# Loading a norm's weight as one row and spreading it over the partitions with TensorE

## The chip, the cores and the metric

The kernel runs on one core of a Trainium2 chip. The time is the device time of one execution in microseconds (us). The core has five engines that run side by side and wait for one another through semaphores: TensorE (PE in the profile; PEld is its loading of weights), VectorE (DVE), ScalarE (ACT), GpSimd (POOL) and SyncE (SP). DMA transfers are issued from the queues of SP, ACT and POOL. A tensor in on-chip memory has 128 partitions; PE writes its results to eight banks of 128 x 512 F32 values, which ACT and DVE can read.

## The reference

One decoder layer for a prompt of 1024 tokens and eight single sample tokens that share weights, 1032 tokens in all, with a model width of 1024. The part that the change touches is the first norm and what uses it at once:

```python
def rmsnorm(x, g):
    xf = x.astype(jnp.float32)
    y = xf * lax.rsqrt(jnp.mean(xf * xf, axis=-1, keepdims=True) + EPS)
    return (y * g.astype(jnp.float32)).astype(x.dtype)

def decoder_layer(x, ...):
    h = rmsnorm(x, g_attn_norm)
    z = h @ w_in
    ...
```

`g_attn_norm` is one vector of 1024 values; every token's row is multiplied by it. `z` has 4360 columns, which are the queries, keys and values of a windowed attention and of a matrix-memory branch (mLSTM), its two gates, and the merge gates. After that come the two branches, their projections and merge, a residual add, a second norm, a gated feed-forward part (1024 to 2816 and back), another residual add and a final norm. The outputs are the normed tokens, the last keys and values, and the states of the matrix memory.

## The kernel before, in words

The 1032 tokens are cut into nine tiles of rows: eight of 128 tokens and one of 8. Tile t is loaded as `x{t}`, [128 tokens, 1024]. The norm of a tile is made in four steps, which are functions of their own:

- `norm_a`: ACT squares the tile and sums each row (`xq`, with the sum in `xss`). `rstd` then makes the mean plus epsilon on DVE (TENSOR_SCALAR) and raises it to the power -0.5 on POOL.
- `norm_b`: one DVE instruction multiplies the tile by its row's factor and by the norm's weight. For that the weight must stand in every partition: `gbc` is a tile [128, 1024] whose rows are all `g_attn`.
- `norm_t`: PE transposes the eight 128 x 128 blocks of the tile against the identity (`cst`, `ident`), four into each of two banks (`xT`).
- `norm_c`: each bank is split into a high and a low part, so that later products can be made in three passes of a shorter format: ACT writes the high part `hh` from the bank, DVE the rest `hl`.

Projections are computed with weights as the stationary operand and the transposed tokens as the moving one, in three chunks of 344 tokens, so that chunk 0 needs tiles 0, 1 and 2. The first product is that of the two mLSTM gates (`if`, the weights are split by ACT into `wl_if`, by DVE into the rest, and spread out by POOL into `wh_if`), the next are `mq` and `mk`.

`start` writes the beginning. SP's queue gets, in this order, tile 0, the weight `gbc`, tiles 1 to 3, and then slices of `w_in` alternating with the tiles 4 to 8. The load of `gbc` reads the one row of 4 KB from memory 128 times:

```python
        for t in range(4):
            x_load(t)
            if t == 0:
                sp.dma_start(gbc, g_attn[0].partition_broadcast(P))
```

Tiles 0, 1 and 2 are normed at once, and the tiles 3 to 8 are normed between the products of the first projections (`side`). While PE has nothing to do, `keep_warm(n)` gives it n products of a tile of zeros (`wz`, 128 x 512, BF16) whose result nobody reads; here they are called fillers. `WARM` holds their numbers: 22 before the first transposes, 3 behind tile 0's, 3 behind tile 1's, 4 behind tile 2's.

PE, SP and POOL take instructions in the order in which the program writes them. The order on ACT and DVE is set by a scheduler. The banks come from pools: `ps_g` (three, for projections and the fillers), `ps_a` (three) and `ps_t` (two).

Of the kernel before, what the change touches and what calls it, by code (L numbers as in the profile page):

```python
# [15 lines left out]
ALU = mybir.AluOpType  # L16
# [4 lines left out]
P = 128  # L21
D = 1024
# [19 lines left out]
PER_M = 4.85  # L42
Z_OFF = [0, 1, 2, 3, 2, 4, 0]
LAST = (4, 5)
WARM = (22, 3, 3, 4)
START = 4
PER_A = 2.95
AHEAD = 3
# [36 lines left out]
def decoder_step(ctx, tc, x_prompt, x_sample, cache_k, cache_v, st_c, st_n, st_m, rel_bias, w_in, b_if, sinks,  # L85
# [3 lines left out]
    pe, act, dve, pool, sp = nc.tensor, nc.scalar, nc.vector, nc.gpsimd, nc.sync  # L89
# [16 lines left out]
    def U(name, dt=F32, shape=None):  # L106
        return up.tile(shape or [P, NT], dt, tag="u", name=name)

    def T(name, shape, dt=F32):
        return tp.tile(shape, dt, tag="t", name=name)  # L110
# [4 lines left out]
    def ps_g(name):  # L115
        return pg.tile([P, 512], F32, tag="g", name=name)
# [17 lines left out]
    dve.memset(nhalf, -0.5)  # L134
    warm = kp.tile([P, 1], F32, name="warm")
    dve.memset(warm, 0.0)
    act.dma_start(cst[:, 0:P], c0[:, 0:P])
    act.activation(warm, warm, AF.Exp)
    gbc = U("gbc", shape=[P, D])
    wz = ep.tile([P, 512], BF16, name="wz")  # L140
    dve.memset(wz, 0.0)
    wps = ps_g("warm")
# [1 line left out]
    def keep_warm(n):  # L144
        for _ in range(n):
            pe.matmul(wps, wz[:, 0:P], wz, start=True, stop=True)

    keep_warm(WARM[0])

    def x_load(t):  # L150
        xt = U(f"x{t}", shape=[P, D])
        sp.dma_start(xt[0:rows[t], :], x_tok[t])
        xs.append(xt)
# [146 lines left out]
    def start(tiles):  # L300
        sl = [p[0] for t in tiles for p in t.prods]
        queue = [w for w in sl if not w.own]
        for t in range(4):
            x_load(t)
            if t == 0:
                sp.dma_start(gbc, g_attn[0].partition_broadcast(P))
        for i in range(FIRST):
            sl[i].load()
            x_load(4 + i)
        x_load(8)  # L310
        loads, splits = queue[2:], queue[2:]
        norm_a(0)
        norm_b(0)
        norm_a(1)
        v0 = norm_t(0)
        keep_warm(WARM[1])
        norm_b(1)
        v1 = norm_t(1)
        keep_warm(WARM[2])
        norm_a(2)  # L320
        norm_c(0, v0)
        norm_b(2)
        v2 = norm_t(2)
        keep_warm(WARM[3])
        norm_c(1, v1)
        sl[0].split()
        norm_c(2, v2)
        sl[1].split()
        loads.pop(0).load()
        loads.pop(0).load()  # L330
        side.add(skewed([(t,) for t in range(3, NB + 1)], [norm_a, norm_b, norm_t, norm_c], [0, 1, 2, 3]), small_loads())
        return sl, loads, splits
# [63 lines left out]
    def norm_a(t):  # L396
        n = rows[t]
        ss = S("xss", [P, 1], 4)
        jk = T(f"xq{t}", [P, D], BF16)
        act.activation(jk[0:n, :], xs[t][0:n, :], AF.Square, accum_out=ss[0:n, :])  # L400
        rstd(ss[0:n, :])
        xs[t] = (xs[t], ss)

    def norm_b(t, _=None):
        n = rows[t]
        xt, ss = xs[t]
        dve.scalar_tensor_tensor(out=xt[0:n, :], in0=xt[0:n, :], scalar=ss[0:n, 0:1], in1=gbc[0:n, :], op0=ALU.mult, op1=ALU.mult)

    def norm_t(t, _=None):
        n = rows[t]  # L410
        xt = xs[t][0]
        vs = []
        for g in range(2):
            tps = (ps_t if t % 2 else ps_a)(f"xT{t}_{g}")
            v = tps.rearrange("p (k t) -> p k t", k=4)[:, :, 0:n]
            for j in range(4):
                pe.transpose(v[:, j], xt[0:n, (4 * g + j) * P:(4 * g + j + 1) * P], ident[0:n, 0:n])
            vs.append(v)
        return vs

    def norm_c(t, vs):
        ts_ = slice(t * P, t * P + rows[t])
        for g in range(2):
            split(hhw[g][:, :, ts_], hlw[g][:, :, ts_], vs[g])
# [330 lines left out]
    def small_loads():  # L755
        pool.dma_start(cst[:, P:], c0[:, P:])
        pool.dma_start(graw[0:8, :], g_ffn.rearrange("o (k p) -> (o k) p", p=P))
        pool.dma_start(graw[8:12, :], g_head.rearrange("o (k p) -> (o k) p", p=P))
        oh = T("oh", [33, 512])
        pool.dma_start(oh, c1)  # L760
        rows_in.append(oh)
        pool.memset(rb[32:33, :], 1.0)
        pool.dma_start(rb[0:32, :], rel_bias)
        pool.dma_start(sink, sinks[0].partition_broadcast(P))
        pool.memset(rst[0:4, :], 1.0)
        pool.memset(rst[0:4, 0:NP].rearrange("p (c t) -> p c t", t=P)[:, :, 0:1], 0.0)
        pool.memset(rw, 0.0)
        pool.dma_start(samp[0], rep(st_n[0].rearrange("b h d -> (b h) d"), 64))
        pool.dma_start(samp[1][:, 2:3], rep(st_m[0].rearrange("b (h o) -> (b h) o", o=1), 1))
        pool.dma_start(sinks_s, sinks[0].rearrange("(h o) -> h o", o=1).unsqueeze(0).to_broadcast([NS, 8, 1]))  # L770
        yield
# [137 lines left out]
    def skewed(units, stages, offs):  # L909
        st = {}  # L910
        for t in range(len(units) + max(offs)):
            for o, f in zip(offs, stages):
                if 0 <= t - o < len(units):
                    u = units[t - o]
                    st[u] = f(*u, st[u]) if u in st else f(*u)
                    yield
# [993 lines left out]
    def hooks_of(i, preps=True):  # L1910
# [12 lines left out]
        if i < NM - 2 and i % 2 == 0 and i >= 2 or i == NM - 1:  # L1923
            def start(i=i):
                p = (KeptPair if i == NM - 1 else Pair)((i - 2) // 2, VL[(i - 2) // 2 * 2], VL[(i - 2) // 2 * 2 + 1])
                main_line(p.s0)
                for j, s in zip(range(2, 7), (p.s1, p.s2, p.s3, p.s4, p.s5)):
                    hk[j].append(ml(s))
            hk[1].append(start)
        if i in (NM, NM + 1):  # L1930
            def start(i=i):
                a, b = u_split(VL[i - 2])
                hk[2].append(ml(a))
                hk[3].append(ml(b))
            hk[1].append(start)
# [176 lines left out]
    for t in tiles[2:FIRST]:  # L2112
        t.prods[0][0].own = True
    run(tiles[:ngate], jobs, *start(tiles[:ngate]))
    gates()
    queue = [w for w in branch if not w.own][2:]
# [151 lines left out]
```

## Time and profile before

| what | before |
|---|---|
| median of 3 runs | 1391.66 us (1391.24 to 1391.66) |
| the profiled execution | 1391.65 us |
| its span | 1389.9 us |
| what lies around the span | 1.75 us |
| PE busy | 1369.4 us, 99% of the span |
| DVE busy | 975.4 us, 70% |
| ACT busy | 617.0 us, 44% |
| POOL busy | 242.0 us, 17% |
| first filler on PE starts | 1.25 us |
| first transposes start | 8.22 us |
| first gate products start | 15.51 us |
| load of `gbc`: issued, to landing | 1.18 us, 5.3 us |

The span is the time from the first to the last recorded instruction; the profiled execution's own time is a little longer. In a view in order of time each row has its start and length in us, the engine, the line of the kernel, the operation, the tile written and the tiles read (buffer numbers left out), their sizes, how many instructions are merged in the row, and in brackets how long the engine had been idle before it and what ended that idle time. The chain of waits follows the work that ended last back to its start. A row of a DMA queue gives packets, MB moved and the share of the 16 DMA engines. The engines PE and PEld are pipelined, so that ends of PE's rows are modelled.

### The profile page before, as it was taken

Reading aid. Unit: us, or ns where it says so; the run is one execution under the profiler, and the core shown is the slowest. Engines: PE = TensorE matmul, PEld = TensorE weight load, DVE = VectorE, ACT = ScalarE, POOL = GpSimd, SP = SyncE. Lnnn points to the kernel's source line nnn. Section 1 sums busy time; section 2 is a strip of 40 time slices with the busy share of each in tenths; the row PEclk is TensorE's granted clock in tenths of the full one; section 3 lists DMA queues with packets and bytes.
Section 4 is the critical chain, followed back from the end, with each engine's and each line's share of the span. In section 5 each row is a group of like instructions: output and inputs, shape, how many; then the busy total and the mean of one; then the engine's idle time right before and its main releaser. Section 6 shows DMA issues by size and latency. Waiting matters only on the chain.

```text
span 1389.9 us, 26966 instructions
## 1 busy us (share of the span) xinstructions
PE 1369.4 (99%) x10723; PEld 1337.9 (96%) x10724; DVE 975.4 (70%) x1853; ACT 617.0 (44%) x1407; POOL 242.0 (17%) x303
## 2 busy tenths in 40 slices
PE   9999999999999999999999999999999999999996
PEld 7999889999999999999999999999999999999996
DVE  7252758886944444755587888898888878888875
ACT  6243567654443331374454343444433343333325
POOL 4012111001111100001132232333333220000003
PEclk9999999999999999999999999999999999999998
DMA  7144224114233274788423344544434468677633
GB/s 224 32 117 113 62 63 100 31 62 149 81 107 100 84 283 137 221 281 283 166 77 120 110 153 153 168 168 139 131 114 144 146 214 304 220 239 237 221 123 122
DMA packets 179173, 208.42 MB, mean 150 GB/s; under 512 B 20638, under 2 KB 137634, under 8 KB 179032
## 3 DMA queue, kind: packets, MB, share of 16 engines
q1 hardware_dynamic: 161928, 151.72, 35.1%
q0 software_dynamic: 16688, 54.40, 10.7%
q8 instruction: 84, 1.38, 0.4%
q10 hardware_dynamic: 432, 0.59, 0.1%
q14 instruction: 41, 0.34, 0.1%
HBM read 140.31 MB, written 68.96 MB: 151 GB/s over the span
## 4 chain that ended last, share of the span: by engine, by line
PE 90%; DVE 3%; ACT 2%; DMA 2%; issue 1%; POOL 0%; SPq 0%; ACTq 0%; POOLq 0%; DVEq 0%
PE af L1589 18%; PE df L1589 9%; PE ad L1589 7%; PE wo L1261 6%; PE bf L1589 5%; PE ag L1589 4%; PE dd L1589 4%; PE o L226 3%; PE mv L226 3%; PE wm L1385 3%; PE wa L1385 3%; PE q L226 3%; PE dg L1589 2%; PE bd L1589 2%; PE mk L226 2%; PE gm L226 2%
## 5 line engine op out<-in xcount | busy, mean ns | idle before, releaser
L125 POOL TENSOR_TENSOR s1f<-s1f,R 128x516 f32<-128x516 f32 x42 | 68.8, 1637 | 87.2 <-DVE s1f L125 71.5
L1589 PE MATMUL df<-Th,op6f 128*128 128x258 f32 x352 | 67.3, 283 | 1.3 <-DVE uu L125 1.3
L1589 PE MATMUL af<-Th,op0f 128*128 128x258 f32 x352 | 67.4, 284 | 0.0
L1589 PE MATMUL bf<-Th,op2f 128*128 128x258 f32 x352 | 67.3, 283 | 0.0
L1589 PE MATMUL df<-Th,op4f 128*128 128x258 f32 x352 | 67.3, 284 | 0.0
L1589 PE MATMUL af<-Th,op1f 128*128 128x258 f32 x352 | 67.1, 283 | 0.0
L1589 PE MATMUL af<-Th,op3f 128*128 128x258 f32 x352 | 66.9, 283 | 0.0
L1589 PE MATMUL af<-Th,op5f 128*128 128x258 f32 x336 | 64.1, 283 | 0.0
L1625 ACT ACTIVATE s1f<-s1f 128x516 f32<-128x516 f32 (+1 forms) x23 | 14.2, 618 | 103.5 <-POOL s1f L125 103.5
L1589 PEld LDWEIGHTS df<-Th,op6f 128*128 128x128 f32 x352 | 55.9, 189 | 1.5 <-DVE uu L125 1.5
L1589 PEld LDWEIGHTS af<-Th,op1f 128*128 128x128 f32 x352 | 56.0, 189 | 0.0
L1589 PEld LDWEIGHTS af<-Th,op0f 128*128 128x128 f32 x352 | 56.0, 189 | 0.0
L1589 PEld LDWEIGHTS bf<-Th,op2f 128*128 128x128 f32 x352 | 56.0, 189 | 0.0
L1589 PEld LDWEIGHTS df<-Th,op4f 128*128 128x128 f32 x352 | 55.8, 189 | 0.0
L1589 PEld LDWEIGHTS af<-Th,op3f 128*128 128x128 f32 x352 | 55.6, 189 | 0.0
L1589 PEld LDWEIGHTS af<-Th,op5f 128*128 128x128 f32 x336 | 53.4, 190 | 0.0
L125 POOL TENSOR_TENSOR s2f<-s2f,R 128x516 f32<-128x516 f32 x21 | 27.4, 1307 | 135.5 <-ACT s2f L1625 135.4
L1589 PE MATMUL bf<-Tl,op2f 128*128 128x258 f32 x176 | 49.8, 283 | 0.0
L1589 PE MATMUL df<-Tl,op6f 128*128 128x258 f32 x176 | 49.7, 282 | 0.0
L1589 PE MATMUL af<-Tl,op1f 128*128 128x258 f32 x176 | 49.7, 282 | 0.0
L1589 PE MATMUL af<-Tl,op0f 128*128 128x258 f32 x176 | 49.7, 282 | 0.0
L1589 PE MATMUL df<-Tl,op4f 128*128 128x258 f32 x176 | 49.7, 282 | 0.0
(690 smaller groups left out, 4935.9 us busy)
## 6 DMA issues: line engine op xcount, KB each, us to landing
ta<-d_t SPq DMA_DIRECT2D x63, 516.0 KB, 6.6
Yd<-in_w_down_dram SPq DMA_DIRECT2D x40, 256.0 KB, 3.5
d_t<-h POOLq DMA_DIRECT2D x18, 516.0 KB, 5.2
d_t<-t POOLq DMA_DIRECT2D x18, 516.0 KB, 4.6
Xf<-in_w_gate_dram SPq DMA_DIRECT2D x22, 256.0 KB, 4.1
Xf<-in_w_up_dram SPq DMA_DIRECT2D x22, 256.0 KB, 6.9
Yf<-in_w_gate_dram SPq DMA_DIRECT2D x22, 256.0 KB, 3.0
Yf<-in_w_up_dram SPq DMA_DIRECT2D x22, 256.0 KB
```

The costliest lines, as they stand in the source:

```text
L125: return eng.tensor_tensor(out=out, in0=a, in1=b, op=op)
L226: pe.matmul(o, a[:, k, :], b[:, cs], start=(k == 0 and i == 0), stop=(k == n - 1 and i == len(passes) - 1))
L1261: pe.matmul(ps[:, th, 0:HB], a[:, k, :], b, start=(k == 0 and i == 0), stop=(k == KD - 1 and i == 2))
L1385: pe.matmul(ps[:, c, 0:CW], a[:, k, :], b[:, cs], start=(k == 0 and q == 0), stop=(k == 3 and q == 2))
L1589: pe.matmul(ps[:, s if ps.shape[1] > 1 else 0, 0:HB], a, b, start=(first and k == 0 and i == 0), stop=(k == self.nk - 1 and i == 2), skip_ ...
L1625: act.activation(s, s, AF.Silu)
```

## The change

The weight is no longer loaded into all partitions. ACT's queue loads it as one row into partition 0 of `gbc` (4 KB), ahead of the identity, and the load in SP's queue between the tiles 0 and 1 is left out. `one` is a row of 128 ones. Two F32 products of TensorE with `one` as the stationary operand and half of the row as the moving one give the weight in every partition, in two banks of `ps_g` (`gain0`, `gain1`). The 22 fillers before the first transposes become 4 ahead of these products and 9 behind them. `norm_b` of the tiles 0, 1 and 2 is made in two halves of 512 columns which read the banks; two ACT copies write the banks to `gbc`, which the tiles 3 to 8 read as before.

```diff
@@ -42,7 +42,7 @@
-WARM = (22, 3, 3, 4)
+WARM = (4, 9, 3, 3, 4)
@@ -134,9 +134,12 @@
     dve.memset(nhalf, -0.5)
     warm = kp.tile([P, 1], F32, name="warm")
     dve.memset(warm, 0.0)
+    gbc = U("gbc", shape=[P, D])
+    act.dma_start(gbc[0:1, :], g_attn)
+    one = T("one", [1, P])
+    dve.memset(one, 1.0)
     act.dma_start(cst[:, 0:P], c0[:, 0:P])
     act.activation(warm, warm, AF.Exp)
-    gbc = U("gbc", shape=[P, D])
     wz = ep.tile([P, 512], BF16, name="wz")
     dve.memset(wz, 0.0)
     wps = ps_g("warm")
@@ -146,6 +149,10 @@
     keep_warm(WARM[0])
+    gps = [ps_g(f"gain{i}") for i in range(2)]
+    for i in range(2):
+        pe.matmul(gps[i], one, gbc[0:1, i * 512:(i + 1) * 512], start=True, stop=True)
+    keep_warm(WARM[1])
@@ -302,8 +309,6 @@
         for t in range(4):
             x_load(t)
-            if t == 0:
-                sp.dma_start(gbc, g_attn[0].partition_broadcast(P))
@@ -313,15 +318,17 @@
         norm_b(0)
         norm_a(1)
         v0 = norm_t(0)
-        keep_warm(WARM[1])
+        keep_warm(WARM[2])
         norm_b(1)
         v1 = norm_t(1)
-        keep_warm(WARM[2])
+        keep_warm(WARM[3])
         norm_a(2)
         norm_c(0, v0)
         norm_b(2)
+        for i in range(2):
+            act.copy(gbc[:, i * 512:(i + 1) * 512], gps[i])
         v2 = norm_t(2)
-        keep_warm(WARM[3])
+        keep_warm(WARM[4])
@@ -404,6 +411,11 @@
     def norm_b(t, _=None):
         n = rows[t]
         xt, ss = xs[t]
+        if t < 3:
+            for i in range(2):
+                cs = slice(i * 512, (i + 1) * 512)
+                dve.scalar_tensor_tensor(out=xt[0:n, cs], in0=xt[0:n, cs], scalar=ss[0:n, 0:1], in1=gps[i], op0=ALU.mult, op1=ALU.mult)
+            return
         dve.scalar_tensor_tensor(out=xt[0:n, :], in0=xt[0:n, :], scalar=ss[0:n, 0:1], in1=gbc[0:n, :], op0=ALU.mult, op1=ALU.mult)
```

What the change does to the order of instructions stands here for the two places at which one engine waits for another. The numbers behind a name tell buffers apart and differ between the two programs. First DVE, from tile 0's norm to tile 1's split (`x_214`, `x_217`, `x_219` are tiles 0 to 2 before, `x_212`, `x_214`, `x_216` in the changed kernel). Before:

```order
L386 TENSOR_SCALAR xss<-xss 128x1
L407 SCALAR_TENSOR_TENSOR x_214<-x_214,xss,gbc 128x1024
L386 TENSOR_SCALAR xss<-xss 128x1
L407 SCALAR_TENSOR_TENSOR x_217<-x_217,xss,gbc 128x1024
L386 TENSOR_SCALAR xss<-xss 128x1
L125 TENSOR_TENSOR hl_126<-xT_0_252,hh_124 128x4x128
L125 TENSOR_TENSOR hl_127<-xT_1_257,hh_125 128x4x128
L407 SCALAR_TENSOR_TENSOR x_219<-x_219,xss,gbc 128x1024
```

In the changed kernel:

```order
L393 TENSOR_SCALAR xss<-xss 128x1
L417 SCALAR_TENSOR_TENSOR x_212<-x_212,xss,gain_109 128x512
L417 SCALAR_TENSOR_TENSOR x_212<-x_212,xss,gain_110 128x512
L393 TENSOR_SCALAR xss<-xss 128x1
L417 SCALAR_TENSOR_TENSOR x_214<-x_214,xss,gain_109 128x512
L417 SCALAR_TENSOR_TENSOR x_214<-x_214,xss,gain_110 128x512
L393 TENSOR_SCALAR xss<-xss 128x1
L125 TENSOR_TENSOR hl_124<-xT_0_250,hh_122 128x4x128
L125 TENSOR_TENSOR hl_125<-xT_1_255,hh_123 128x4x128
L417 SCALAR_TENSOR_TENSOR x_216<-x_216,xss,gain_109 128x512
L417 SCALAR_TENSOR_TENSOR x_216<-x_216,xss,gain_110 128x512
```

Each norm product of the three tiles is now two instructions of 512 columns that read a bank written by PE; the order is otherwise the same, here and in the rest of the program.

Then ACT, from tile 2's squares (`xq`) to tile 1's high parts (`hh`) and the gate weights. Before:

```order
L400 ACTIVATE xq_280,xss<-x_219 128x1024
L231 ACTIVATE hh_124<-xT_0_252 128x4x128
L231 ACTIVATE hh_125<-xT_1_257 128x4x128
L231 ACTIVATE hh_124<-xT_0_266 128x4x128
L231 ACTIVATE hh_125<-xT_1_271 128x4x128
L231 ACTIVATE wl_if<-ws_if 128x64
```

In the changed kernel:

```order
L407 ACTIVATE xq_279,xss<-x_216 128x1024
L238 ACTIVATE hh_122<-xT_0_250 128x4x128
L238 ACTIVATE hh_123<-xT_1_255 128x4x128
L329 COPY gbc<-gain_109 128x512
L329 COPY gbc<-gain_110 128x512
L238 ACTIVATE hh_122<-xT_0_265 128x4x128
L238 ACTIVATE hh_123<-xT_1_270 128x4x128
L238 ACTIVATE wl_if<-ws_if 128x64
```

The two copies from the banks to `gbc` stand between tile 0's and tile 1's high parts; at the beginning of ACT's order the load of `gbc` stands ahead of the load of the identity. On PE the two products (L154) stand behind the fourth filler, and nine fillers stand between them and tile 0's transposes. On every engine all that follows is the same row by row.

## The prediction

> **What bounds the kernel now.** I read the page's totals first, then the chain of waits over the first 60 us, then each engine in order of time up to 20 us.
>
> ```profile
> span 1389.9 us, 26966 instructions
> PE 1369.4 (99%) x10723; PEld 1337.9 (96%) x10724; DVE 975.4 (70%) x1853; ACT 617.0 (44%) x1407; POOL 242.0 (17%) x303
> ```
>
> PE is the bound nearly everywhere, so a change ahead of the first real product is worth what it moves the start of the unbroken PE stream. Where that stream starts, and what leads to it, stands in the chain (start, length, what):
>
> ```profile
> 1.18 0.42 SPq L306
> ...
> 1.65 6.28 DMA x<-in_x_prompt_dram
> ...
> 7.96 1.16 ACT xq L400 x2
> ...
> 9.96 1.28 DVE x L407
> ...
> 12.51 1.20 DVE x L407
> 13.71 0.04 issue
> 13.76 1.09 PE xT L417 x8
> 14.85 0.05 issue
> 14.90 0.81 PE warm L146 x3
> 15.71 2.60 PE if L218 x16
> ```
>
> The chain passes the issue of the gain load on SP's queue, waits for token tile 1, then goes through the norm of tiles 1 and 2 on DVE to the gate products at 15.71. From there PE is in the chain almost without a break. So the change has to be priced on the 15.7 us before that. DVE in order of time:
>
> ```profile
> 6.88 1.28 DVE L407 SCALAR_TENSOR_TENSOR x<-x,xss,gbc 128x1024 f32<-128x1024 f32 x1 [0.68 <-POOL xss L125]
> 9.14 0.15 DVE L386 TENSOR_SCALAR xss<-xss 128x1 f32<-128x1 f32 x1 [0.97 <-ACT xq L400]
> 9.96 1.28 DVE L407 SCALAR_TENSOR_TENSOR x<-x,xss,gbc 128x1024 f32<-128x1024 f32 x1 [0.67 <-POOL xss L125]
> ...
> 11.23 1.28 DVE L125 TENSOR_TENSOR hl<-xT,hh 128x512 fp32r<-128x512 f32 x2
> 12.43 1.27 DVE L407 SCALAR_TENSOR_TENSOR x<-x,xss,gbc 128x1024 f32<-128x1024 f32 x1
> 13.62 1.28 DVE L125 TENSOR_TENSOR hl<-xT,hh 128x512 fp32r<-128x512 f32 x2
> 14.82 0.22 DVE L125 TENSOR_TENSOR wl_if<-ws_if,wl_if 128x64 fp32r<-128x64 f32 x1
> ...
> 18.76 1.28 DVE L407 SCALAR_TENSOR_TENSOR x<-x,xss,gbc 128x1024 f32<-128x1024 f32 x1
> ```
>
> Two things: DVE idles 0.97 us before 9.14 because tile 1 came late; from 9.96 on it is busy without a gap, through the product of tile 2 and the split of the gate weights (wl_if). ACT and POOL in order of time:
>
> ```profile
> 4.87 1.06 ACT L400 ACTIVATE xq<-x 128x1024 bf16<-128x1024 f32 x1 [2.19 <-DMA x<-in_x_prompt_dram]
> ...
> 7.96 1.06 ACT L400 ACTIVATE xq<-x 128x1024 bf16<-128x1024 f32 x1 [1.94 <-DMA x<-in_x_prompt_dram]
> ...
> 9.23 1.06 ACT L400 ACTIVATE xq<-x 128x1024 bf16<-128x1024 f32 x1
> ...
> 10.29 1.06 ACT L231 ACTIVATE hh<-xT 128x512 fp32r<-128x512 f32 x2
> 12.00 1.08 ACT L231 ACTIVATE hh<-xT 128x512 fp32r<-128x512 f32 x2 [0.65 <-PE xT L417]
> ```
>
> ```profile
> 9.37 0.56 POOL L125 TENSOR_TENSOR xss<-xss,nhalf 128x1 f32<-128x1 f32 x1 [2.52 <-DVE xss L386]
> ...
> 15.10 0.36 POOL L255 CAST wh_if<-wl_if 128x32 fp32r<-128x32 f32 x2 [1.18 <-DVE wl_if L125]
> ```
>
> ACT waits for tile 0 until 4.87 and for tile 1 until 7.96. POOL's cast of the gate weights ends at 15.46, with the last filler of PE; both release the gate products.
>
> **Removed: 512 KB ahead of tile 1.** The gain load stands in SP's queue between tiles 0 and 1. What that queue (q1) had moved by 4.87 us (tile 0 landed), 6.5 (gain: issued at 1.18, 5.3 us to landing) and 7.93 (tile 1), as packets, MB, share, one row for each window from 0:
>
> ```profile
> q1 hardware_dynamic: 205, 0.77, 51.5%
> ```
>
> ```profile
> q1 hardware_dynamic: 336, 1.25, 58.2%
> ```
>
> ```profile
> q1 hardware_dynamic: 498, 1.84, 66.2%
> ```
>
> A 512 KB load is 0.524 MB. Tile 0 lands with 0.77 MB moved, the gain with 1.25 (1.05 needed), tile 1 with 1.84 (1.57 needed): each lands when the queue is 0.20 to 0.27 MB past it. Without the gain load tile 1 needs 1.25 to 1.3 MB and lands near 6.5 us instead of 7.93, tile 2 near 7.9. SP's issue of 0.42 us goes too. All later loads move up by the same 1.4 us; none of them bounds the stretch that follows.
>
> **Added on PE.** Before: 22 fillers. Now 4, two F32 products of one row of ones with the gain row, 9 fillers. The products wait for the row, and behind them in PE's order stand the fillers and tile 0's transposes; ACT and DVE wait for those. The fillers now, their pace (weight loads, start and length) and the first transposes:
>
> ```profile
> 1.25 7.10 PE L146 MATMUL warm<-wz 128*128 128x512 bf16 x22 [1.25 <-DVE wz L141]
> ...
> 5.49 0.15 PEld L146 LDWEIGHTS <-wz 128*128 128x128 bf16 x1 [0.28 <-issue]
> 5.81 2.04 PEld L146 LDWEIGHTS <-wz 128*128 128x128 bf16 x10 [0.17 <-issue]
> 8.22 0.86 PEld L417 LDWEIGHTS xT<-cst,x 128*128 128x128 f32 x8 [0.37 <-DVE x L407]
> ```
>
> A filler takes 0.43 us before 5.8 us (the 11 that start from 1.25), and 0.21 after it: the array runs at half pace at first. The granted clock in the windows reads 1.00 throughout and does not show this.
>
> The nearest F32 product in the trace is the bias table's, 384 columns as two rows at full pace:
>
> ```profile
> L779 PE MATMUL bt<-oh,rb x2: 483/484/486, 68.1 to 68.4; 33*8 33x384 f32 x2
> ```
>
> The two rows start 0.3 us apart and cover 0.8 us in all, about 0.65 of streaming and a tail of 0.16. For 512 columns that is 0.87 us of streaming at full pace, 1.74 at half.
>
> When does the row land? The load is issued first on ACT's queue, near 0.74 us. Bounds: two small gain loads on POOL's queue at 31.6 us took 2.0 to 2.3 us, hence 2.8 to 3.0; the two tiny bias loads on POOL's queue, issued in the same crowded start, took 5.4 to 6.0, hence 6.1 to 6.7. The rows of both, and of what ACT's queue (q10, the identity in 144 packets) had moved by 2.75 and by 4.87 us:
>
> ```profile
> DMA to landing us min/median/max: 2.0/2.1/2.3
> ```
>
> ```profile
> DMA to landing us min/median/max: 5.4/5.7/6.0
> ```
>
> ```profile
> q10 hardware_dynamic: 4, 0.00, 0.2%
> ```
>
> ```profile
> q10 hardware_dynamic: 144, 0.07, 4.6%
> ```
>
> The same queue's first packets passed just before 2.75 us, and the row now goes ahead of them: I take 3.2 us. Then the first product is done near 3.2+1.74+0.16 = 5.1, the second near 6.8 at half pace, 6.3 if the pace rises at 5.8 as now. DVE needs the first at 6.88 and the second at 7.5, so they cost nothing; the cover is 0.7 us. The 9 fillers (9x0.21 = 1.9 us) end between 8.2 and 8.7, where the 22 end now (8.2). ACT takes the transposes only when tile 2's squares are done, near 9.1, so up to 0.5 us of lateness is hidden.
>
> **Added on DVE and ACT.** The norm product of tiles 0 to 2 becomes two halves of 512 that read a bank. The nearest row with a bank as source is hl<-xT: 1.28 us for two of 512, the same as one of 1024 from memory. I price the split at 0. A gain: transposes 0 to 3 of a tile can start 0.64 us earlier. The copy of both banks to memory is two ACT copies of 512, about 1.06 us as hh<-xT for the same shape; they stand after tile 0's hh and before tile 1's hh, where ACT idles 0.65 us now. The matrix of the gain is needed in memory by tile 3 only (18.76 now, the copies end near 11.2). The memset of the ones (0.06 us on DVE) is before any work. ACT issues the identity's load and its table load one DMA issue (0.4 us) later; ACT waits 2.19 us for tile 0, and the identity, complete by 4.87 now, is needed at 8.2, so nothing.
>
> **Sum, in the order of time.** Tile 0's norm product starts at 6.88 as now and ends at 8.16. Tile 1's squares are done near 7.7, no longer late: DVE's next step starts at 8.16 instead of 9.14. It is now DVE that sets it, so of the 1.4 us won on the load 1.0 is left. POOL's power 8.35 to 8.9, tile 1's product 8.95 to 10.2 (9.96 now, -1.0). ACT: tile 2's squares 7.95 to 9.1, tile 0's hh 9.1 to 10.15. DVE: tile 0's hl 10.3 to 11.5, tile 2's product 11.5 to 12.75 (12.43 now, -0.95), tile 1's hl from 12.7; its hh is ready at 12.3 (transposes at 11.2, copies until 11.2, then 1.08), 0.4 us of cover for the copies. wl_if at 13.9 (14.82 now), POOL's cast done at 14.5, gate products at 14.55 instead of 15.51. PE is free by then: tile 2's transposes end near 13.3, the four fillers at 14.1. From 14.5 on the order of PE, DVE and ACT is the same row by row, so the 0.95 us stay.
>
> The profiled run took 1391.65 us, beside a median of 1391.66: one and the same. 1391.65 - 0.95 = 1390.7 us. Without the other terms the case runs from -0.3 (row at 4.5) to -1.5 (the load's whole gain).
>
> **Rivals.**
>
> 1. *PE reaches tile 0's transposes late* (slower). The place is the start of those transposes. Break-even: ACT's hh starts at 10.29 now, which half the transposes precede by 0.5 us, so from 9.7 on the gain is gone. Price by the late bound: row at 6.4, PE idle since 3.0 and so at half pace, products until 10.0, 9 fillers at first at half pace until 12.1, transposes until 12.9; hh starts near 12.6, tile 2's product near 14.6 instead of 12.43: about +2.1, 1393.7 us. With a row at 3.2 but half pace until 10, fillers end at 10.4 and the sum is about +0.3. For it: no product on PE waits for a load at this place now, and the half pace lasts until 5.8 as it is. Against: ACT's queue moves packets by 2.75.
> The Trainium skill ("TensorE: Matmul & The Clock Gate", Part 1: The HAM clock gate) says the pace doubles after a free-running window of about 3.4 us of sustained activity, and that idling loses it. By that rule a gap at 3.0 could push the rise to a later window, which is this rival's mild end (0.08 of its chance); the trace's rise at 5.81, 4.56 us after the first filler, fits it.
>
> 2. *The start moves and the end doesn't*: a wait later in the program that doesn't hang on the start takes the time back. The chain does hold long DMA waits:
>
> ```profile
> 147.64 6.83 DMA kq<-d_int
> ```
>
> But that one reads rows written by the kernel itself behind PE's products, so it moves along. Time: 1391.6.
>
> 3. *More than forecast*: if banks are read faster than memory and the earlier half transposes shift tile 0's and 2's splits too, the start moves by the queue's full 1.4 us and up to 0.6 for the halves: -2.0, 1389.6 us. Against: DVE's string of products doesn't shrink by any row here.
>
> **How the numbers follow.** Forecast 0.58, rival 1 0.2, rival 2 0.1, rival 3 0.12. The likeliest gives 1390.7, by itself 1390.1 to 1391.4. Taking in rival 2, rival 3 down to its middle and the mild half of rival 1: 1389.8 to 1392.6. A measurement of this kernel tells about 0.2%, 2.8 us, from no change. Every case priced above lies within that; beyond it are only a rival 1 worse than its late bound (0.04) and an effect that I don't see on the faster side (0.03). So faster 0.03, same 0.93, slower 0.04.
>
> **What would show it.** Right: tile 1's squares start near 6.5 and tile 1's product near 8.95, the gain products end before 7.5, transposes of tile 0 start before 9, gate products near 14.55, and one constant shift afterwards. Wrong: DVE waiting for PE (gain) before tile 0's product, fillers at 0.43 us behind the products, ACT's first hh after 10.3, or a shift that is not the same at 75 us and at the end.

## Result and the profile after

The changed kernel takes 1396.96 us (median of 6 runs, 1394.78 to 1398.54) beside 1391.66 us before (1390.88 to 1392.07 in the same comparison): a ratio of 1.0037, 95% interval 1.0024 to 1.0050. It is 5.3 us slower, where 1390.7 had been forecast and 1392.6 was the range's upper end. A second set of 6 runs of the same kernel gave 1395.40 beside 1392.01, 1.0030 (1.0018 to 1.0042): 3.4 us slower. The profiled execution of the changed kernel took 1395.29 us.

The page's totals after:

```profile
span 1393.1 us, 26972 instructions
PE 1372.9 (99%) x10718; PEld 1339.5 (96%) x10719; DVE 975.5 (70%) x1857; ACT 618.3 (44%) x1409; POOL 242.6 (17%) x303
```

PE has 3.5 us more busy time with 5 matmuls and 5 weight loads fewer, so some of its work went slower. Where is told by the chain of waits of the first 21 us (start, length, what):

```profile
1.38 1.89 PE warm L149 x4
3.27 3.71 PE gain L154 x4
6.97 3.95 PE warm L149 x9
10.93 1.72 PE xT L429 x8
...
12.67 0.61 ACT hh L238
...
13.91 1.41 DVE x L417 x2
...
15.34 0.58 ACT gbc L329
...
16.31 0.61 ACT hh L238
...
17.06 0.68 DVE hl L125
...
18.36 2.80 PE if L225 x16
```

The load of token tile 1, which led this chain before, is gone from it. PE leads it from the first filler to tile 0's transposes, then tile 2's norm product on DVE, then the copies of the gain on ACT. The same stretch by engine in order of time, PE and then DVE and ACT:

```profile
3.19 0.50 PEld L154 LDWEIGHTS gain<-gbc,one 1*128 1x128 f32 x2 [0.84 <-DMA gbc<-in_g_attn_norm_dram]
3.20 3.78 PE L154 MATMUL gain<-gbc,one 1*128 1x512 f32 x4
6.91 4.02 PE L149 MATMUL warm<-wz 128*128 128x512 bf16 x9
10.72 1.92 PE L429 MATMUL xT<-cst,x 128*128 128x128 f32 x8
...
18.36 1.53 PE L225 MATMUL if<-hh,wh_if 128*128 128x344 f32 x8 [1.41 <-POOL wh_if L262]
```

```profile
8.82 1.41 DVE L417 SCALAR_TENSOR_TENSOR x<-x,xss,gain 128x512 f32<-128x512 f32 x2 [0.67 <-POOL xss L125]
11.82 0.60 ACT L238 ACTIVATE hh<-xT 128x512 fp32r<-128x512 f32 x1 [2.79 <-PE xT L429]
13.91 1.40 DVE L417 SCALAR_TENSOR_TENSOR x<-x,xss,gain 128x512 f32<-128x512 f32 x2
14.68 1.24 ACT L329 COPY gbc<-gain 128x512 f32<-128x512 f32 x2 [1.41 <-DVE x L417]
16.45 1.29 DVE L125 TENSOR_TENSOR hl<-xT,hh 128x512 fp32r<-128x512 f32 x2 [1.15 <-ACT hh L238]
```

Three things are to be seen. The row of the gain lands at 3.19 and both products are done at 6.98. The nine fillers behind them take 4.02 us, 0.43 each, half pace, and tile 0's eight transposes are as slow (1.92 us instead of 1.09 at full pace); ACT waits 2.79 us for them and starts its first split at 11.82, 1.53 us later than before (10.29). Then ACT's copies stand at 14.68: they wait 1.41 us for DVE's norm product of tile 2, which reads the same banks, and tile 1's split stands behind them; DVE idles 1.15 us. The gate products start at 18.36 instead of 15.51.

So the start is 2.85 us late. Against the profile before, the same rows of PE (beginning of `gps`, 65.4 us before, and so on) are 2.8 us late at 65 us, 2.9 at 197, 3.2 from 497 us to the end; outside the span lie 2.2 us instead of 1.75. That is 3.6 us for this execution. The first set's median, 5.3 us, says that other executions lose more. The profiled execution of the second set (1398.51 us) shows where: 1.9 us late at 65, 3.5 at 197, 6.4 from 696 us on. The change also brought losses that come and go, hundreds of microseconds behind its place.

### The profile page after: what moved, and what is told of

Read it like the earlier page. It is cut to its first block, busy times and chain, and to the rows that moved or that the text cites. A ratio compares the mean times of both kernels' runs of the same rounds, so it can differ in the third digit from the quotient of the medians.

```text
span 1393.1 us, 26972 instructions
## 1 busy us (share of the span) xinstructions
PE 1372.9 (99%) x10718; PEld 1339.5 (96%) x10719; DVE 975.5 (70%) x1857; ACT 618.3 (44%) x1409; POOL 242.6 (17%) x303
## 4 chain that ended last, share of the span: by engine, by line
PE 91%; DVE 3%; ACT 2%; DMA 1%; issue 1%; POOL 0%; SPq 0%; ACTq 0%; POOLq 0%; DVEq 0%
PE af L1601 18%; PE df L1601 9%; PE ad L1601 7%; PE wo L1273 6%; PE bf L1601 5%; PE ag L1601 4%; PE dd L1601 4%; PE o L233 3%; PE mv L233 3%; PE wm L1397 3%; PE wa L1397 3%; PE q L233 3%; PE dg L1601 2%; PE bd L1601 2%; PE mk L233 2%; PE gm L233 2%
```

## Experiments

There were two theories at the outset. A: products of one row do not raise PE's pace, whatever their type; the half pace then lasts through fillers and transposes. B: F32 products (or the wait for their row) are what holds the pace, or the pace costs nothing and the copies are the loss. In the table, "gate" is the start of the gate products in the profiled execution (15.51 before), "at 65" how much later than before the row of `gps` starts there, "time" the median less that of the kernel before, run beside it. There is one profile for each row, so single places can differ from execution to execution, as the first two rows show.

| kernel | gate, us | at 65, us | time, us | ratio (95%) |
|---|---|---|---|---|
| the change | 18.36 | +2.8 | +5.3 | 1.0037 (1.0024 to 1.0050) |
| the change again | 17.43 | +1.9 | +3.4 | 1.0030 (1.0018 to 1.0042) |
| p1 one-row F32 stand-ins | 16.77 | +1.3 | +4.0 | 1.0026 (1.0017 to 1.0036) |
| p2 128-row F32 stand-ins | 15.43 | -0.1 | +3.9 | 1.0023 (1.0015 to 1.0032) |
| p3 one-row BF16 stand-ins | 15.61 | +0.1 | +0.5 | 1.0003 (0.9994 to 1.0011) |
| p4 64-row BF16 stand-ins | 16.24 | +0.7 | +0.3 | 1.0002 (0.9993 to 1.0011) |
| c1 copies late | 16.74 | +1.8 | +4.9 | 1.0033 (1.0020 to 1.0045) |
| c2 fillers first | 17.49 | +1.9 | +3.3 | 1.0025 (1.0015 to 1.0035) |
| c3 both | 15.33 | +0.4 | +4.4 | 1.0032 (1.0020 to 1.0043) |
| q1 before, 17 fillers | 15.52 | 0.0 | +1.9 | 1.0012 (1.0004 to 1.0021) |
| q2 p2, count restored | 15.50 | 0.0 | +0.3 | 1.0002 (0.9993 to 1.0011) |
| q3 change, count restored | 18.23 | +2.7 | +3.4 | 1.0023 (1.0014 to 1.0032) |
| q4 c3, count restored | 16.25 | +1.3 | +1.7 | 1.0013 (1.0004 to 1.0021) |
| r1 q3 with copies late | 16.61 | +1.6 | +2.7 | 1.0020 (1.0011 to 1.0030) |
| r2 r1, gain over 128 rows | 17.25 | +2.3 | +4.4 | 1.0030 (1.0020 to 1.0040) |
| r3 r2, row earlier | 15.28 | +0.3 | +1.7 | 1.0013 (1.0004 to 1.0022) |
| r4 before, 5 products more | 15.48 | 0.0 | -0.2 | 1.0000 (0.9991 to 1.0009) |

### The pace, with stand-ins in the kernel before

Four kernels are the kernel before with 4 fillers, then products of zeros where the gain products would stand, then 9 fillers. p1 and p2 also clear a tile of F32 zeros on DVE; nothing else differs.

p1, and p2 with `zf[:, 0:P], zf` in place of the one row:

```diff
-    keep_warm(WARM[0])
+    zf = ep.tile([P, 512], F32, name="zf")
+    dve.memset(zf, 0.0)
+    keep_warm(4)
+    for _ in range(2):
+        pe.matmul(wps, zf[0:1, 0:P], zf[0:1, :], start=True, stop=True)
+    keep_warm(9)
```

p3, and p4 with 64 rows:

```diff
-    keep_warm(WARM[0])
+    keep_warm(4)
+    for _ in range(8):
+        pe.matmul(wps, wz[0:1, 0:P], wz[0:1, :], start=True, stop=True)
+    keep_warm(9)
```

> The kernel before, with its 22 fillers replaced by 4 fillers, two F32 products of ONE row (zeros, nothing loaded, nothing waited for) and 9 fillers. Theory A (products of one row do not count as work for TensorE's pace): the pace is still half behind them, the 9 fillers run at 0.43 us each, first transposes after 10 us, rise of the pace not before 9.8 us, total 1 to 5 us over the kernel before and spread over some us. Theory B (what lost the pace is the wait for the loaded row): nothing waits here, rise near 5.8 us, total within 0.5 us of before. Theory C (F32 products of any height do not count): as A, and the run with 128 rows too.

> The same with the two F32 products over 128 rows of zeros. Theory A: they count, the pace rises near 5.8 us, the 9 fillers take 0.21 us each, total within 0.5 us of before. Theory B: the same. Theory C: as the one-row run, 1 to 5 us slower.

> The same with 8 BF16 fillers of ONE row in place of the two F32 products (same length). Theory A: as the one-row F32 run, half pace past 9.8 us, 1 to 5 us slower than before. Theories B and C: within 0.5 us of before.

> The same with 8 BF16 fillers of 64 rows. If the count goes by the share of rows with a threshold under one half, as before within 0.5 us; if it needs more, as the one-row runs. Theories B and C: as before.

PE in order of time, the stand-ins and the nine fillers of p1, of p2, of p3 and of p4, for p1 and p2 with tile 0's transposes:

```profile
3.07 3.78 PE L152 MATMUL warm<-zf 1*128 1x512 f32 x4
6.78 4.02 PE L146 MATMUL warm<-wz 128*128 128x512 bf16 x9
10.59 1.82 PE L422 MATMUL xT<-cst,x 128*128 128x128 f32 x8
```

```profile
2.93 2.42 PE L152 MATMUL warm<-zf 128*128 128x512 f32 x4
5.19 2.11 PE L146 MATMUL warm<-wz 128*128 128x512 bf16 x9
8.31 1.09 PE L422 MATMUL xT<-cst,x 128*128 128x128 f32 x8 [1.02 <-DVE x L412]
```

```profile
3.07 3.59 PE L150 MATMUL warm<-wz 1*128 1x512 bf16 x8
6.59 3.63 PE L146 MATMUL warm<-wz 128*128 128x512 bf16 x9
```

```profile
3.07 3.59 PE L150 MATMUL warm<-wz 64*128 64x512 bf16 x8
6.59 4.02 PE L146 MATMUL warm<-wz 128*128 128x512 bf16 x9
```

PE has no gap from the stand-ins to the end of the fillers in any of them. With stand-ins of 128 rows the fillers behind take 0.21 us each from 5.19 on; with one row, F32 or BF16, and with 64 rows too they stay at 0.43 us. It is therefore the number of rows, not the type and not a wait for a load: theory A, and wider than I had it, since half the rows do no better than one. The trace's record of clock changes has the rise at 12.2 us in p1, 9.7 in p3 and 11.0 in p4, 3.1 to 5.4 us after the 128-row fillers resume. In the kernel before it has it at 5.7, 4.4 us after the first filler. (The windows, which read 1.00 from the start, do not show this first rise.) All 18 profiles agree: in the eight in which products of one or 64 rows follow the first four fillers the rise is at 9.7 to 12.8 us, in the ten others at 4.0 to 7.2. The Trainium skill ("TensorE: Matmul & The Clock Gate", Part 1: The HAM clock gate) has the pace rise after a free-running window of about 3.4 us of sustained work; these delays are of that size, and what the runs add is which products count as work.

The half pace costs the start 1.2 us in p1, 0.7 in p4 and 0.1 in p3: the later the rise, the more. So p3 and p4, which I had expected 1 to 5 us over if A held, stay within 0.5 us of the kernel before. But p2, whose start is as before, takes 3.9 us more all the same. That could not come from the pace.

### Copies and order in the changed kernel

The change again, unaltered (a0). c1 moves the copies behind the split of the first `mq` weights, c2 puts all 13 fillers ahead of the gain products (so that PE reaches them at full pace), c3 does both:

```diff
-WARM = (4, 9, 3, 3, 4)
+WARM = (13, 0, 3, 3, 4)
...
         norm_b(2)
-        for i in range(2):
-            act.copy(gbc[:, i * 512:(i + 1) * 512], gps[i])
...
         sl[1].split()
+        for i in range(2):
+            act.copy(gbc[:, i * 512:(i + 1) * 512], gps[i])
```

> The changed kernel once more, as the control for the three that follow. Theory: half pace until 10 to 16 us in the profile, gate products 2 to 5 us later than the 15.5 of before, total 3 to 7 us over before, spread over some us from run to run.

> The changed kernel with the two ACT copies of the banks put behind the split of the first mq weights. Theory D (the copies hold ACT until tile 2's product has read the bank, and tile 1's high parts stand behind them): tile 1's high parts start right after its transposes, DVE's 1.15 us gap before tile 1's hl is gone, gate products 1.0 to 1.3 us earlier than in the changed kernel, total about 1.1 us less, so still 2 to 4 us over before. Rival (the late transposes alone set the time): no difference to the changed kernel beyond 0.3 us.

> The changed kernel with all 13 fillers ahead of the two products. Theory A: the pace rises during the fillers, near 6 us, the products run in about 1.1 us each from 6.4 us, tile 0's second half waits for the second product until about 8.3 us, transposes at full pace; gate products near 16.5, total 0 to 1.5 us over before and little spread. If the products themselves or the wait were what costs: as the changed kernel, 3 to 7 us over.

> Both edits: 13 fillers first and the copies late. If pace and copies are all that the forecast missed: gate products near 15.3, total within 0.7 us of before, on either side; otherwise 2 us or more over.

PE of c2 in order of time:

```profile
6.96 1.98 PE L154 MATMUL gain<-gbc,one 1*128 1x512 f32 x4
8.99 1.51 PE L429 MATMUL xT<-cst,x 128*128 128x128 f32 x8
10.29 1.49 PE L149 MATMUL warm<-wz 128*128 128x512 bf16 x3
11.57 1.91 PE L429 MATMUL xT<-cst,x 128*128 128x128 f32 x8
```

The gain products now run at full pace, 1.98 us for both. But two products of one row and eight transposes later, at 10.2, the pace is lost: three fillers take 1.49 us and tile 1's transposes 1.91. The Trainium skill ("TensorE: Matmul & The Clock Gate", Part 4: PE-mode transpose) says that full pace does not engage for transposes, which do not count as busy in the same way; c2 agrees, without telling them from the one-row products. c3 tells more. Its fillers end at 6.1 us and its transposes start at 8.07, and the clock falls at 8.4 (third figure from the end):

```profile
8.00:9.00 1.00, 0.95 (x6) 0.60 (x6) 0.83 (x3) 0.93 (x3) 0.05 (x1) 0.69 1.24 266
```

Only 0.3 us of transposes lie before the fall, so here it is the one-row products (6.04 to 8.02): they do not only fail to raise the pace, they let it fall. c2 and c3 get it back 3.4 us later.

c1's gate products start 0.7 us before those of the change again and 1.6 before those of the first profile, but its time is no better (+4.9). c2 was expected at 0 to 1.5 us over and is at 3.3. c3 shows the largest gain at the start: gate products at 15.33, earlier than before, since tile 0's transposes start at 8.07 and tile 1's split no longer stands behind the copies. Its time is 4.4 us above the kernel before nevertheless.

So the losses at the start can be taken away, and the time stays. The profile of c3 shows where it went: it is 0.4 us late at 65, 0.3 at 197, 0.8 at 497, 2.6 at 696, 3.2 at the end.

### Ten PE instructions fewer

What p2 and c3 share with the change, and p3, p4 with the kernel before, is PE's count of instructions ahead of the first transposes. A filler is a weight load and a matmul; an F32 product counts two of each. The change has 13 fillers and 2 F32 products for 22 fillers, 10 instructions fewer; so have p1, p2, c1 to c3. p3 and p4 have 21 products, 2 fewer. q1 does nothing but make 22 fillers 17, which also leaves PE idle for 1.2 us ahead of tile 0's transposes. q2 to q4 give p2, the change and c3 their count back, with products of a single column behind the fillers (five, in q4 six and one filler fewer):

```diff
-WARM = (22, 3, 3, 4)
+WARM = (17, 3, 3, 4)
```

```diff
     keep_warm(9)
+    for _ in range(5):
+        pe.matmul(wps[:, 0:1], wz[:, 0:P], wz[:, 0:1], start=True, stop=True)
```

> The kernel before with 17 fillers instead of 22: ten fewer instructions on PE ahead of everything else, no product of one row, no wait, no loaded row. Theory E (PE's instructions are fetched in blocks of 16 KB as it goes through them; ten fewer ahead put every later fetch some tenths of a us later against the work, and the one near 671 us then comes behind the issue of the reload of w_out's slices and holds it up): start unchanged within 0.3 us, the fetch near 672.0 us or later, a new wait of PE near 680 us of 1.5 to 2.6 us, up to 1.4 us more near 190 us, total 2 to 4 us over before, spread like the other slow ones. Rival (the late jumps come from the F32 products or from chance): within 0.5 us of before.

> The run with two F32 products over 128 rows, plus five products of one column (10 instructions, about 0.7 us of PE in its slack), which restore the number of PE's instructions. Theory E: back to before within 0.5 us, where it was 3.9 us slower without them. Rival (F32 products as such): still 3 to 4 us slower.

> The changed kernel with the same five products of one column behind its nine fillers. Theory E with A and D: the start stays 2 to 3 us late (half pace, copies), the jumps near 190 and 680 us go: total 2 to 3.5 us over before, about 2 us less than the changed kernel. Rival: no less than the changed kernel.

> Fillers ahead of the products, copies late, and the number of PE's instructions restored (12 fillers, 6 products of one column). Theory: start within 0.7 us of before, no later jumps, total within 0.8 us of before, where the same without the restored number was 4.4 us slower. Rival: 3 us or more over.

q1 is 1.9 us slower with an unmoved start, and q2 takes back 3.6 of p2's 3.9 us, q4 2.7 of c3's 4.4. The count thus sets a loss of 2 to 4 us in these, with an idle gap ahead of tile 0's transposes (q1, p2) and without one (c3). For the change it is less: q3's median is 3.4 us above before, as in the second set of the change, but its runs lie between 1394.0 and 1395.9, where the change's lie between 1394.5 and 1398.5.

How it arises is partly seen. The chain of q1 near 190 us, beside that of the kernel before:

```profile
189.50 0.55 PE mkt L567 x2
190.04 1.72 PE q L226 x6
191.76 1.60 PE my L579 x8
```

```profile
188.75 0.44 PE mkt L567 x2
189.19 0.94 PE q L226 x6
190.13 0.89 PE my L579 x8
```

The same rows take nearly twice the time. The windows of q1 give the granted clock (third figure from the end):

```profile
189.00:190.00 1.00, 0.50 (x3) 0.50 (x4) 0.00 (x0) 1.00 (x5) 0.00 (x0) 0.84 0.07 16
190.00:191.00 1.00, 1.00 (x6) 1.00 (x5) 0.99 (x2) 1.00 (x3) 0.00 (x0) 0.50 0.00 0
192.00:194.00 2.00, 2.00 (x16) 1.76 (x15) 1.35 (x6) 0.00 (x0) 0.84 (x1) 0.73 0.74 199
```

PE idles 0.91 us ahead of `mvt` and 1.62 ahead of `mkt` here, where the kernel before idles only 0.88 in all; then the clock is 0.50 for 3.4 us (0.3 us of the window to 190, 2.0 us to 192, 1.1 us of the last), and the two rows of the chain take 1.5 us longer (3.32 instead of 1.83). The profiles of q1, of the change's second set and of c1 show the drop; that of p2 has 2.3 us of idle time without it, so the idle time alone does not decide. Why PE waits longer there is not settled: the chain leads back to round trips of rows through memory that start between 146 and 178 us and are 5.9 to 8.3 us long from kernel to kernel.

The other place is near 671 us. The chain of p2, and of q2, which differs by the five one-column products:

```profile
665.32 7.39 PE wo L1266 x60
...
672.92 7.17 DMA wl_wo5b<-d_wo
...
680.23 9.81 PE wo L1266 x80
```

```profile
664.39 25.64 PE wo L1268 x213
```

In q2 the stream is unbroken; in p2 a reload of weights lands too late, and PE waits. SP issues that reload as two loads, `wh_wo5b` and `wl_wo5b`. The second one's issue, in SP's order of time, in the kernel before and in p2:

```profile
672.36 0.37 SPq L205 DMA_DIRECT2D wl_wo5b<-d_wo  x1
```

```profile
672.92 0.97 SPq L210 DMA_DIRECT2D wl_wo5b<-d_wo  x1
```

It takes 0.6 us longer. What lies beside it is on the DMA queues, a single packet of 16 KB of instructions, in the kernel before in the window 671 to 672 and in p2 in the window 672 to 673:

```profile
q8 instruction: 1, 0.02, 5.8%
```

```profile
q8 instruction: 1, 0.02, 5.9%
```

In all 18 profiles the start of this packet stands against SP's issue of the first of the two loads as follows (a negative figure is a packet behind the issue):

| kernels | packet ahead of the issue, us | second issue takes, us | lost between 672 and 685 us |
|---|---|---|---|
| before, p4, q2, q3, q4, r1 to r4 | 0.51 to 1.27 | 0.37 to 0.66 | 0 to 0.1 |
| p3, the change's first profile | 0.16 | 0.66, 0.80 | 0 |
| p1, q1 | -0.01, -0.03 | 0.88, 0.89 | 0.4, 0.3 |
| the change again, p2, c1, c2, c3 | -0.40 to 0.08 | 0.97 to 1.22 | 1.2 to 2.5 |

There is a loss in the seven profiles whose packet starts less than 0.1 us ahead of the issue or behind it, and none in the eleven others; how large it is the distance does not tell, since p1 and q1 lie among the rest. With the count of before or more the distance is 0.53 us or more in every profile, with ten PE instructions fewer 0.16 or less. That is the link between the count and this loss, as far as profiles can show it; the packet was not moved without the count, so that it is the cause is not shown.

### A version without the two losses

r1 is q3 with the copies late. r2 makes the gain products 128 rows high: the gain tile is cleared, its row 0 loaded, and the stationary operand is zero but for a row of ones; 8 fillers stand ahead and 5 behind. r3 clears the tile on POOL first thing, so that the load is issued earlier, with 10 fillers ahead and 3 behind. r4 is the kernel before with five one-column products more, 10 PE instructions too many instead of too few. The main lines of r3's edit of the change (r2 has `dve.memset(gbc, 0.0)` behind the tile of zeros; in both the identity's load goes ahead of the row's):

```diff
-    act.dma_start(gbc[0:1, :], g_attn)
-    one = T("one", [1, P])
-    dve.memset(one, 1.0)
...
+    pool.memset(gbc, 0.0)
+    act.dma_start(gbc[0:1, :], g_attn)
...
+    one = T("one", [P, P])
+    dve.memset(one, 0.0)
+    dve.memset(one[0:1, :], 1.0)
...
-        pe.matmul(gps[i], one, gbc[0:1, i * 512:(i + 1) * 512], start=True, stop=True)
+        pe.matmul(gps[i], one, gbc[:, i * 512:(i + 1) * 512], start=True, stop=True)
```

> The change with ACT's copies of the banks put behind the second gate-weight split, and five products of one column behind the fillers, so that PE has as many instructions ahead of its first transposes as before. Two causes are held apart here: the start (half pace, copies) and the later jumps that went with ten PE instructions fewer. If the copies cost about 1.1 us of the start and the later jumps are gone with the count, the gate products start near 17 (18.2 with the copies in place and the same count), the shift is 1.3 to 1.8 at 65 us and no more than 0.6 above that at the end: 1393.2 to 1394.2. If the copies cost nothing, the time is that of the change with the count alone, 1395.1, and the gate products stay at 18.2.

> As the kernel beside it (copies late, count as before), but the gain products span all 128 rows: the gain tile is cleared first, its row 0 loaded, and the stationary operand is zero but for a row 0 of ones, so the two products give the same banks. Eight fillers stand ahead, five behind. If what keeps PE at half pace is that a product of one row does not count as work, the pace rises between 4 and 6 us, tile 0's transposes are done by 9.2, the gate products start at 14.5 to 15.7 (15.71 before) and the time is 1390.5 to 1392.2, what had been predicted of the change. If it is the F32 products as such or the wait for the row, the pace rises at 9 us or later and the time is that of the kernel beside it, 1393 to 1394.

> As the changed kernel with full-height gain products, late copies and the PE count of before, but the gain tile is cleared on POOL at the very start, so that the row's load is issued near 1.4 us instead of 2.3, and ten fillers stand ahead of the products, three behind. If the row lands by 5.6, PE has no gap, the pace rises near 5.7 as before, the products end by 7.5, the gate products start at 14.6 to 15.7 (15.71 before) and the time is 1390.5 to 1392.2. If the row is late again (after 6 us) or the pace still rises only at 9 us or later, the gate products start at 16.5 or later and the time is 1393.5 to 1395.5.

> The kernel before with five products of one column added behind its 22 fillers: ten PE instructions more, where seventeen fillers were ten fewer and cost 1.9 us by jumps at 188 to 197 us and later. The five cost 0.3 us ahead of tile 0's transposes, which have 1.2 us of cover, so the start stays (gate products at 15.71). If what costs there is a fetch of PE's instructions falling into a bad place, moving it the other way is neutral: 1391.0 to 1392.4, no jump at 188 us. If any other number of instructions is worse than the 22 fillers' own, it costs 1 to 3 us too: 1392.8 to 1394.8.

r1: the gate products start 1.6 us earlier than in q3, which is what the copies held up; 0.6 of that is lost by 65 us, so 1.0 remains there and 0.6 of the medians, whose intervals overlap. Where it is lost is shown by the chain of r3, in which the late copies stand ahead of tile 3's squares:

```profile
15.91 0.96 ACT gbc L339 x2
16.88 1.26 ACT xq L411 x3
```

In all six kernels with late copies, c1, c3, q4 and r1 to r3, the lateness at 65 us is 0.5 to 0.6 us worse than that of the gate products. In r3 ACT is full from 14.8 us on, and the 1.06 us of copies have no free place.

r2 is a miss that tells something. Its row, issued at 2.30 behind token tiles, lands at 6.9. PE in order of time, and windows:

```profile
6.90 2.49 PE L156 MATMUL gain<-gbc,one 128*128 128x512 f32 x4 [2.06 <-DMA gbc<-in_g_attn_norm_dram]
```

```profile
7.00:8.00 1.00, 1.00 (x3) 0.52 (x4) 0.00 (x0) 0.79 (x3) 0.00 (x0) 1.00 1.07 389
8.00:9.00 1.00, 1.00 (x2) 0.18 (x2) 0.75 (x1) 0.67 (x2) 0.00 (x0) 0.60 1.23 291
9.00:10.00 1.00, 1.00 (x3) 0.30 (x2) 0.57 (x1) 0.00 (x0) 0.00 (x0) 0.50 0.98 366
```

Eight fillers had raised the pace at 4.8 us; it was lost at 8.2, and 2.06 of the 3.4 us between were idle. The Trainium skill ("TensorE: Matmul & The Clock Gate", Part 1: The HAM clock gate) lets the pace go after an idle window of about 3.4 us; here 2.06 us were enough.

r3 has the pace: its row lands near 5.9, the products take 1.95 us, tile 0's transposes start at 8.58 at full pace, the gate products at 15.28. Its fillers raise the pace at 4.5 us, as c3's do at 5.0; behind products of 128 rows it stays (three fillers follow them), where c3 lost it behind products of one row. That bears A out inside the changed kernel. It does not reach the forecast. The row comes 2.7 us later than in the change, so that DVE's first norm product waits 1.12 us for the gain and starts at 7.22 instead of 6.88. The gate products gain 0.23 us instead of 0.95, the copies take 0.5 back by 65 us, and the median is 1.7 us above before. r4 equals the kernel before: ten PE instructions more do not hurt as ten fewer do.

## Why the prediction was wrong

Point by point, in the order of its steps.

- **The load removed: right.** Tile 1's squares start at 6.04 (forecast near 6.5) and its norm product at 8.82 (8.95, before 9.96). The row lands at 3.19 (3.2). The gain this should bring, 0.95 us, was there at 8.82 (1.14 us) and was gone at 11.82.
- **The gain products: right in size.** Half pace, 1.9 us each and done at 6.98 (1.74 and 6.8); DVE does not wait for them.
- **"The 9 fillers (9x0.21 = 1.9 us) end between 8.2 and 8.7": the step that failed first.** They took 4.02 us and tile 0's transposes 1.92. I took the pace to rise near 5.8, "as now", and so let one-row products count as what the fillers had been. p1 to p4 show that they do not. What came is rival 1's mild end, half pace until 10, which I priced at +0.3; the pace came at 10.3 (second profile) and 12.8 us (first), and p1, which has only that of the change, is 1.2 us late. Rival 1 named a late row as its cause, and the row was not late.
- **"the copies end near 11.2", 0.4 us of cover: the second.** I let them wait for the gain products alone. Each started only when DVE's last read of the same bank was over (14.68 and 15.34 us); they end near 15.9 and hold up tile 1's split: 1.15 us of DVE's time, 1.0 of the kernel's at 65 us (q3 against r1). Even with the pace right the place was wrong, since tile 2's norm product was forecast until 12.75.
- **The split priced at 0: mis-sized.** Two halves that read a bank take 1.40 us and the one of 1024 from memory took 1.28, 0.12 us a tile.
- **"From 14.5 on the order of PE, DVE and ACT is the same row by row, so the 0.95 us stay": the third.** In the first profile the shift is near constant (2.8 to 3.2 us), in the second it jumps by 1.7 us near 190 and by 2.5 near 671. I had priced the start only, and had not asked what else depends on the number of instructions. In the first profile the start alone, 2.85 us late, is outside every case that I priced, up to the late bound of rival 1 at +2.1; in the second the start is 1.9 us late, within that bound, and the jumps carry the time beyond it.
- **Rival 2 looked in the right region.** It named a round trip through memory at 147.64 us and dismissed it, because it moves along with PE. It does move along, but its length does not stay: 6.83 us there, 5.92 in the change's second profile, where the next such trip takes 7.66 instead of 7.04. That a loss lay there was not foreseen; the rival expected the start's gain to be taken back.

For the first set: in its profiled execution the start is 2.85 us late. Of this the half pace makes about 1.2, as in p1, and the copies most of the rest: between q3 and r1, which differ in nothing else, 1.6 at the gate products and 1.0 at 65 us. The median of 5.3 us leaves 2.4 for what came later; the profiled execution has 0.8 of it, 0.4 of that outside the span.

The count is not all there is to it. r1, r2 and r3 have the count of before and lose 1.1, 2.1 and 1.3 us more behind 65 us. The profiles place part of this. Late copies have a price there too: in c1, c3, q4, r1 and r3 0.6 to 0.7 us more is lost between 696 us and 1380 (0.4 in r2), where no kernel with early copies or none loses more than 0.1; so it is for each of the pairs q3 and r1, c2 and c3, the change and c1. The time outside the span is 2.3 and 2.4 us in r2 and r3 instead of 1.75. The rest of r2's loss is not in its profile, which is of one of its fastest executions (1394.53 us). Why these places lose stays open.

## What to carry to other kernels

Where fillers keep PE's pace up, ask of every product put among them how many rows it has: here one row, and even 64, did not raise the pace, and what followed ran at half pace until 3 to 6 us of full-height products had gone by. Where a copy of a bank waits for the other engine's last read of that bank, as here, place it behind that read in the order, where its engine has room. An edit that changes the number of instructions ahead of a tight stream can move the time by a few microseconds without touching the rest of the work; restore the count to see what the edit itself is worth.

## What the runs showed that was not expected

- Products of 64 rows leave PE at half pace as those of one row do (4.02 us for nine fillers behind them, 2.11 behind two F32 products of 128 rows).
- Five fillers fewer at the start of a 1391 us kernel cost 1.9 us (q1, 1.0012, 1.0004 to 1.0021), and five one-column products gave p2 3.6 us back (q2); five more in the kernel before changed nothing (r4).
- One-row products let a pace that was already reached fall again, from 8.4 to 11.8 us in c3, though PE had been busy for 95% of every microsecond or more.
- A 16 KB packet of instructions that started less than 0.1 us ahead of SP's issue of a load, or just behind it, went with the next issue taking 0.88 to 1.22 us instead of 0.37, and with 0.3 to 2.5 us lost on PE.
- About 2.5 us of idling near 188 us went with a halved granted clock for 3.4 us in q1, in the midst of a kernel in which PE is busy 99% of the span; 2.3 us did not in p2.
- A row of 4 KB took 2.5 us to land when its load was issued first (0.74 to 3.19), 4.2 when issued at 1.7 (r3) and 4.6 when issued at 2.3 (r2), behind the token tiles.
